# A hybrid decoder layer on one core: the second MLP product in seven block products instead of eight, and a low part made by an adding DMA

## The chip, the cores and the metric

The kernel runs on one core of one Trainium2 chip. The metric is the device time in microseconds of one execution. The time before is the median of three runs, 508.71 us (508.6 to 509.68). The profile is of a single execution.

## The reference, cut to what matters

One layer of a decoder trunk on 256 tokens of width 1024, in float32: a combined input projection, a convolution branch and a sparse attention branch with gates, a cross-attention over 256 memory tokens, and an MLP with squared ReLU. The change touches the MLP:

```
h = h + CrossAttn(RMSNorm(h), RMSNorm(mem))      # 4 heads over N_MEM memory tokens
hf = _rmsnorm(h, norm_ffn_g) @ w_ff1             # (256, 1024) @ (1024, 4096)
h = h + jnp.square(jax.nn.relu(hf)) @ w_ff2      # (256, 4096) @ (4096, 1024)
return _rmsnorm(h, norm_final_g)
```

## The kernel before, in words

**Products in three parts.** TensorE multiplies most operands in the format fp32r. Each operand is split into a high part (a copy in fp32r, by ScalarE) and a low part (the rest, subtracted by VectorE), and a product that stands for the float32 one is the sum of three: high x high, high x low, low x high (`mm3`, line 322).

**The stream of weights.** All weights lie in HBM in chunks of 128 x 2048 floats (1 MB) in the order of `STREAM` (line 38): after the cross-attention come first-product chunks 0 and 1, then alternately first-product chunk i + 2 and second-product chunk i. SP loads them (`load`, line 185) into three buffers, `raw`. Each chunk is split in two halves of 1024 columns: `high` (line 211) allocates a high and a low tile from two pools of `HALVES` = 6 buffers and puts out ScalarE's copy; its `low` puts out VectorE's subtraction, and after the second half loads the next chunk. `split_high` (line 227) starts a half only while fewer than `HALVES - held[0]` are prepared and unused, and `weights` (line 238) hands a prepared half to the product that needs it.

**The order of the work.** The whole order is written by the program: each engine executes its instructions in the order in which Python puts them out. The helper `Counted` (line 66) adds up a price for each instruction of TensorE, VectorE and ScalarE, and `split_ahead`, `meanwhile` and `tick` (lines 252 to 297) use these sums to decide when to put out the next high part, low part or waiting job. Jobs that take several steps are generators, which `tick` advances one step each. All instructions of these engines carry line 87, the line of the helper.

**The MLP.** `f2` holds the scaled input, transposed, in high and low parts (tile name ff). `ff1(c)` (line 1273) computes 256 of the 4096 hidden features as two tiles of 128 features x 256 tokens (`form_b`, `tile_b`, lines 327 to 349). In the wide form that is used here one matmul of 512 columns multiplies the high weights by the high and low input side by side, and one of 256 columns the low weights by the high input, for each of 8 steps: 16 matmuls a tile. The PSUM banks (tile ps_f) rotate over four. `activation` (line 1260): ScalarE copies one half of the bank to ft, VectorE adds the other, squares with ReLU, ScalarE copies the high part to fs, VectorE subtracts the low part. `ff2` (line 1291) multiplies: for chunk c, for each of the two 128-row blocks of hidden features, each 128-token half and each 512-column half of the output, three matmuls of 512 columns: 24 a chunk, summed over all 16 chunks in four PSUM banks (ps_ff). The loop at line 1327 puts out first-product chunk c + 2, then second-product chunk c. The last two chunks are multiplied output half by output half, so that adding the residual (h_rm, transposed from h_t by TensorE in four steps of `ff_scale`, line 1240), the final norm and the stores start before the last product is done; the last one is split at column 768 (`edge`). `g_out`, the final gain, is loaded by SP before the MLP.

The convolution earlier in the kernel (lines 564 to 600) already sums some of its taps by DMAs that GpSimd's queue issues with an add (`added`, line 580), of 256 KB each.

Of the kernel before, what the change touches and what calls it, by code (L numbers as in the profile page):

```python
# [16 lines left out]
P = 128  # L17
D = 1024
# [44 lines left out]
EARLY = (3,)  # L63

# [41 lines left out]
def block_kernel(ctx, tc, x, xt, mem, memt, wst, wki, vecs, convw, gout, out):  # L106
# [75 lines left out]
    nload, dma = [0], [0.0]  # L182
    high_jobs, low_jobs = [], []

    def load(cuts=(0, N_CHUNK), before=lambda q: None):
        if nload[0] >= len(STREAM):
            return
        c = nload[0]
        nload[0] += 1
        key = STREAM[c]  # L190
        raw = t8(f"raw{c}", F32, (P, N_CHUNK)) if c in EARLY else raws.tile([P, N_CHUNK], F32, tag="raw", name=f"raw{c}")
        n = KT * NK if key[0] == "ki" else N_CHUNK
        src = wki if key[0] == "ki" else wst[INDEX[key]]
        for q, ns in enumerate(slice(a, min(b, n)) for a, b in zip(cuts, cuts[1:])):
            before(q)
            nc.sync.dma_start(raw[:, ns], src[:, ns])
            dma[0] += 1.3 * (ns.stop - ns.start)
        parts = 1 if key[0] == "ki" else 2
        for q in range(parts):
            ns = slice(q * n // parts, (q + 1) * n // parts)  # L200
            high_jobs.append(lambda ns=ns, q=q, last=q == parts - 1: high(key, c, raw, ns, q, last))

    def load_keys(q):
        if q == 0:
            nload[0] += 1
            whole["xk", 0] = raws.tile([P, N_CHUNK], F32, tag="raw", name="raw0").rearrange("p (k n) -> p k n", k=2 * KT)
        both = whole["xk", 0].rearrange("p (c k) n -> p c k n", c=2)
        src = wst[INDEX["xk", 0]].rearrange("p (c k n) -> p c k n", c=2, k=KT)
        nc.sync.dma_start(both[:, :, 4 * q : 4 * q + 4, :], src[:, :, 4 * q : 4 * q + 4, :])

    def high(key, c, raw, ns, q, last):
        n = ns.stop - ns.start
        hi = highs.tile([P, N_CHUNK // 2], F32R, tag="hi", name=f"hi{c}_{q}")[:, :n]
        lo = lows.tile([P, N_CHUNK // 2], F32R, tag="lo", name=f"lo{c}_{q}")[:, :n]
        act(hi, raw[:, ns], AF.Copy)
        ready = scalar.total + 100

        def low():
            dve.after(ready)
            dve.tensor_tensor(out=lo, in0=raw[:, ns], in1=hi.bitcast(F32), op=ALU.subtract)  # L220
            prepared[(*key, q)] = (hi, lo)
            if last and c not in EARLY:
                load()

        low_jobs.append(low)

    def split_high():
# [8 lines left out]
    nsplit, nused, held = [0], [0], [1]  # L236

    def weights(kind, i, half, kt):

        key = (kind, i, half)  # L240
        while key not in prepared:
            split_high()
# [41 lines left out]
    def tick():  # L284
# [9 lines left out]
        if scalar.total < pe.total - SPARE or len(low_jobs) < 2:  # L294
            split_high()
        dve.total = max(dve.total, pe.total - 2900)
        scalar.total = max(scalar.total, pe.total - 2900)

    nturn, groups, halves, due, later = [0], [], [], [], []

# [577 lines left out]
    def qk(name):  # L878
        return big.tile([P, 2, S], F32, tag="qk", bufs=4, name=name)

    for i in range(4):
        q, k = qk(f"q{i}"), qk(f"k{i}")
# [329 lines left out]
    form_c("xo", 0, dst, ox2, 0)  # L1212
    lows_of = []
# [22 lines left out]
    g_out = t8("g_out", F32, (P, D))  # L1236
    nc.sync.dma_start(g_out, gout.partition_broadcast(P))
    r2 = []

    def ff_scale():  # L1240
# [7 lines left out]
        yield  # L1248
        r2.append(sq_f.by_row([ps_aux(f"ps_ff{rb}")[:, :2] for rb in range(2)], [sq_f.sums[:, 0, :]], -1))
        for rb in range(2):  # L1250
            for hf in range(2):
                yield
                ps = ps_aux(f"ps_hr{rb}{hf}")
                for j in range(4):
                    pe.transpose(ps[:, j * P : j * P + P], h_t[:, 4 * hf + j, rb * P : rb * P + P], ident)
                act(h_rm[:, rb, hf * 512 : hf * 512 + 512], ps, AF.Copy)

    start(ff_scale())

    def activation(ps, ct, sh, sl):  # L1260
        t = w2(f"ft{ct}", F32, (P, S))
        total(t, ps)

        def square():
            dve.scalar_tensor_tensor(out=t, in0=t, scalar=0.0, in1=t, op0=ALU.max, op1=ALU.mult)
            act(sh, t, AF.Copy)

        due.append(square)
        yield
        yield  # L1270
        dve.tensor_tensor(out=sl, in0=t, in1=sh.bitcast(F32), op=ALU.subtract)

    def ff1(c):
        parts = t8(f"fs{c}", F32R, (P, 4, S))
        jobs = []

        def after(ct, ps):
            jobs.append(start(activation(ps, ct, parts[:, ct % 2, :], parts[:, 2 + ct % 2, :])))

        if c == 0:  # L1280
            form_b_late("f1", c, f2, after, (4,), ps_aux)
        else:
            form_b("f1", c, f2, after)
        return parts[:, :2, :], parts[:, 2:, :], jobs

    tags[:] = [("mm", 2), ("mm", 2), ("aux", 2), ("aux", 2)]
    turns[0] = -1
    pending = [ff1(0), ff1(1)]
    dst = [[ps_acc(f"ps_ff{rb}{hf}") for hf in range(2)] for rb in range(2)]

    def ff2(c, k, w, x2, rb, hf, cs=slice(0, 512), ps=None):
        x2 = Parts(*x2[:2])
        rows, cols = slice(rb * P, rb * P + P), slice(hf * 512 + cs.start, hf * 512 + cs.stop)
        first, last = c == 0 and k == 0, c == 15 and k == 1
        if ps is None:
            ps = dst[rb][hf][:, cs]
        else:
            first = c == 14 and k == 0
        mm3(ps, x2.hi(k)[:, rows], x2.lo(k)[:, rows], w[0][:, 0, cols], w[1][:, 0, cols], first, last, cs.start > 0)

    hg = t8("hg", F32, (P, 2, D))
# [3 lines left out]
    def last_sum(rb, ps, lo, hi):  # L1305
        h = h_rm[:, rb, lo:hi]
        dve.scalar_tensor_tensor(out=h, in0=ps, scalar=r2[0][:, rb : rb + 1], in1=h, op0=ALU.mult, op1=ALU.add)
# [8 lines left out]
    def power_of(rb, n, other):  # L1316

        dve.tensor_tensor(out=ss[:, rb, n : n + 1], in0=ss[:, rb, n : n + 1], in1=ss[:, rb, other : other + 1], op=ALU.add)
        raised(rb, n)

# [6 lines left out]
    for c in range(14):  # L1327
        pending.append(ff1(c + 2))
        *x2, jobs = pending.pop(0)
        for job in jobs:  # L1330
            finish(job)
        for k in range(2):
            w = weights("f2", c, k, 1)
            split_ahead()
            for rb in range(2):
                for hf in range(2):
                    ff2(c, k, w, x2, rb, hf)
            tick()
    for *_, jobs in pending:
        for job in jobs:  # L1340
            finish(job)
    ws = {(c, k): weights("f2", c, k, 1) for c in (14, 15) for k in range(2)}

    def last_products(rb, lo, hi, ps=None):
        for (c, k), w in ws.items():
            ff2(c, k, w, pending[c - 14], rb, lo // 512, slice(lo % 512, lo % 512 + hi - lo), ps)

    for hf in range(2):
        lo, hi = 512 * hf, 512 * hf + 512
        last_products(0, lo, hi)  # L1350
        last_sum(0, dst[0][hf], lo, hi)
        squared(0, hf, lo, hi)
        if hf == 1:
            dve.tensor_scalar(ss[:, 0, 0:1], ss[:, 0, 0:1], EPS, None, ALU.add)
        gained(0, lo, hi)
    power_of(0, 1, 0)
    scale = rs[:, 0:1]
    for n, (lo, hi) in enumerate(((0, 352), (352, D))):
        cols = hg[:, 0, lo:hi]
        if n == 0:  # L1360
            act(cols, cols, AF.Copy, scale=scale)
        else:
            dve.tensor_scalar(cols, cols, scale, None, ALU.mult)
        store(0, n, lo, hi)

    last_products(1, 0, 512)
    last_sum(1, dst[1][0], 0, 512)
    squared(1, 0, 0, 512)
    gained(1, 0, 512)
    last_products(1, 512, 768)  # L1370
    edge = ps_aux("ps_edge")[:, :S]
    last_products(1, 768, D, edge)
    last_sum(1, dst[1][1], 512, D)
    squared(1, 1, 512, 768)
    gained(1, 512, 768)
    dve.scalar_tensor_tensor(out=ss[:, 1, 1:2], in0=ss[:, 1, 1:2], scalar=EPS, in1=ss[:, 1, 0:1], op0=ALU.add, op1=ALU.add)
    last_sum(1, edge, 768, D)
    junk = w2("junk_edge")
    dve.tensor_tensor_reduce(out=junk[:, :S], in0=h_rm[:, 1, 768:], in1=h_rm[:, 1, 768:], scale=1.0 / D, scalar=ss[:, 1, 1:2],
# [3 lines left out]
    dve.tensor_scalar(hg[:, 1, 432:768], hg[:, 1, 432:768], scale, None, ALU.mult)  # L1383
    store(1, 1, 432, 768)
    act(hg[:, 1, :432], hg[:, 1, :432], AF.Copy, scale=scale)
    store(1, 0, 0, 432)
    dve.scalar_tensor_tensor(out=hg[:, 1, 768:], in0=h_rm[:, 1, 768:], scalar=scale, in1=g_out[:, 768:], op0=ALU.mult, op1=ALU.mult)
    store(1, 2, 768, D)
# [69 lines left out]
```

## Time and profile before

| | |
|---|---|
| median of 3 runs | 508.71 us |
| the profiled execution | 508.7 us, its span 506.9 us |
| granted TensorE clock, mean | 0.997 |
| TensorE busy | 498.8 us (98%) |
| VectorE busy | 410.6 us (81%) |
| ScalarE busy | 332.8 us (66%) |
| GpSimd busy | 44.0 us (9%) |
| the MLP's products, first to last on the chain | 321.7 to 500.9 us |

How to read it: in the lists, PE is TensorE, PEld its weight loads, DVE VectorE, ACT ScalarE, POOL GpSimd, SP the queue that issues most DMAs. A group of instructions reads "line engine operation out<-in shapes xcount | busy us, mean ns of one | idle us before, and who ended it". A wait reads "who <- what it waited for: us in total, times, longest". In the timeline the first two columns are start and duration in us.

### The profile page before, as it was taken

Reading aid. Unit: us, or ns where it says so; the run is one execution under the profiler, and the core shown is the slowest. Engines: PE = TensorE matmul, PEld = TensorE weight load, DVE = VectorE, ACT = ScalarE, POOL = GpSimd, SP = SyncE. Lnnn points to the kernel's source line nnn. Section 1 sums busy time; section 2 is a strip of 40 time slices with the busy share of each in tenths; the row PEclk is TensorE's granted clock in tenths of the full one; section 3 lists DMA queues with packets and bytes.
Section 4 is the critical chain, followed back from the end, with each engine's and each line's share of the span. In section 5 each row is a group of like instructions: output and inputs, shape, how many; then the busy total and the mean of one; then the engine's idle time right before and its main releaser. Section 6 shows DMA issues by size and latency. Waiting matters only on the chain.

```text
span 506.9 us, 7744 instructions
## 1 busy us (share of the span) xinstructions
PE 498.8 (98%) x2893; PEld 439.1 (87%) x2893; DVE 410.6 (81%) x795; ACT 332.8 (66%) x605; POOL 44.0 (9%) x64
## 2 busy tenths in 40 slices
PE   8999999999999999999999999999999999999995
PEld 6999999888889898888888888988888888888884
DVE  4989999999999998798999984787765666665555
ACT  4867666887889977887768474666544454545432
POOL 1001122232323210000000000000000000000000
PEclk9999999999999999999999999999999999999998
DMA  8968869999999984474755444344655545555302
GB/s 295 390 264 254 245 170 214 235 262 254 295 270 278 232 221 167 154 261 143 273 172 198 173 171 177 149 166 167 248 187 221 174 165 180 222 185 195 133 0 83
DMA packets 20869, 104.50 MB, mean 206 GB/s; under 512 B 2400, under 2 KB 3040, under 8 KB 10464
## 3 DMA queue, kind: packets, MB, share of 16 engines
q1 hardware_dynamic: 14496, 92.83, 51.5%
q0 software_dynamic: 5904, 10.75, 12.1%
q8 instruction: 22, 0.36, 0.3%
q10 hardware_dynamic: 432, 0.44, 0.2%
q14 instruction: 15, 0.12, 0.1%
HBM read 92.21 MB, written 1.05 MB: 184 GB/s over the span
## 4 chain that ended last, share of the span: by engine, by line
PE 97%; issue 1%; DVE 0%; ACT 0%; POOLq 0%; POOL 0%; DVEq 0%
PE ps_f L87 18%; PE ps_ff L87 16%; PE ps_conv L87 9%; PE ps_ao L87 4%; PE ps_mix L87 4%; PE ps_co L87 4%; PE ps_ga L87 4%; PE ps_k L87 4%; PE ps_gc L87 4%; PE ps_q L87 4%; PE ps_v L87 4%; PE ps_xo L87 3%; PE ps_xk L87 3%; PE ps_xq L87 2%; PE ps_qi L87 2%; PE ps_xv L87 2%
## 5 line engine op out<-in xcount | busy, mean ns | idle before, releaser
L87 DVE TENSOR_TENSOR lo<-raw,hi 128x1024 fp32r<-128x1024 f32 x163 | 196.9, 1215 | 3.4 <-ACT hi L87 3.4
L87 ACT ACTIVATE hi<-raw 128x1024 fp32r<-128x1024 f32 x163 | 169.9, 1049 | 25.5 <-PE ps_ff L87 18.4
L87 PE MATMUL ps_ff<-hi,fs 128*128 128x512 f32 (+1 forms) x256 | 80.6, 387 | 0.0
L87 PE MATMUL ps_f<-ff,hi 128*128 128x512 f32 x256 | 64.4, 392 | 0.0
L87 DVE SCALAR_TENSOR_TENSOR acc<-u,cw,acc 128x249 f32<-128x249 f32 (+17 forms) x150 | 62.6, 467 | 0.0
L87 DVE TENSOR_TENSOR ft<-ps_f,ft 128x256 f32<-128x256 f32 x32 | 13.6, 424 | 53.1 <-ACT ft L87 53.0
L87 PEld LDWEIGHTS ps_ff<-hi,fs 128*128 128x128 f32 x256 | 47.9, 188 | 9.4
L87 PEld LDWEIGHTS ps_f<-ff,hi 128*128 128x128 f32 x256 | 46.6, 188 | 8.7
L87 PE MATMUL ps_ff<-lo,fs 128*128 128x512 f32 (+1 forms) x128 | 49.5, 387 | 0.0
L87 PE MATMUL ps_conv<-n,hi 128*128 128x256 f32 x256 | 46.6, 284 | 0.0
L580 POOL DMA_DIRECT2D added<-prod x41 | 35.7, 870 | 120.9 <-ACT prod L87 46.5
L87 PEld LDWEIGHTS ps_conv<-n,hi 128*128 128x128 f32 x256 | 39.9, 192 | 0.8 <-issue 0.7
L87 ACT ACTIVATE prod<-u,cw 128x226 f32<-128x226 f32 (+10 forms) x82 | 35.0, 475 | 5.0 <-DMA added<-prod 5.0
L87 PEld LDWEIGHTS ps_f<-ff,lo 128*128 128x128 f32 x256 | 35.2, 190 | 2.7
L87 PE MATMUL ps_conv<-n,lo 128*128 128x256 f32 x128 | 36.2, 283 | 0.0
L87 PE MATMUL ps_f<-ff,lo 128*128 128x256 f32 x256 | 36.0, 282 | 0.0
L87 ACT ACTIVATE fs<-ft 128x256 fp32r<-128x256 f32 x32 | 13.4, 419 | 31.1 <-DVE ft L87 31.1
L87 PEld LDWEIGHTS ps_ff<-lo,fs 128*128 128x128 f32 x128 | 24.1, 188 | 4.3
L87 ACT ACTIVATE ft<-ps_f 128x256 f32<-128x256 f32 x32 | 12.2, 380 | 20.6 <-PE ps_f L87 19.4
L87 PEld LDWEIGHTS ps_conv<-n,lo 128*128 128x128 f32 x128 | 24.6, 192 | 0.0
L87 PE MATMUL ps_v<-hi,n 128*128 128x512 f32 x64 | 19.9, 389 | 0.0
L1322 POOL TENSOR_TENSOR rs_o<-ss_o,half 128x1 f32<-128x1 f32 x2 | 1.1, 558 | 214.5 <-DVE ss_o L87 214.5
(244 smaller groups left out, 891.5 us busy)
## 6 DMA issues: line engine op xcount, KB each, us to landing
raw<-in_wst_dram SPq DMA_DIRECT2D x79, 1024.0 KB, 4.9
added<-prod POOLq DMA_DIRECT2D x41, 256.0 KB, 8.6
raw<-in_wst_dram SPq DMA_DIRECT2D x6, 512.0 KB, 8.9
mem_t<-in_memt_dram SPq DMA_DIRECT2D x2, 512.0 KB, 5.2
x_rm<-in_x_dram SPq DMA_DIRECT2D x2, 512.0 KB, 8.4
mem_rm<-in_mem_dram SPq DMA_DIRECT2D x1, 1024.0 KB, 5.1
mem_t<-in_memt_dram SPq DMA_DIRECT2D x1, 1024.0 KB, 7.1
h_t<-in_xt_dram SPq DMA_DIRECT2D x1, 1024.0 KB, 8.0
```

The costliest lines, as they stand in the source:

```text
L87: return fn(*args, **kwargs)
L580: nc.gpsimd.dma_start(added[:, ts, :].rearrange("p t n -> p (t n)"), prod[:, self.n, :, :].rearrange("p t n -> p (t n)"), accum_op=ALU.add)
L1322: nc.gpsimd.tensor_tensor(out=rs[:, rb : rb + 1], in0=ss[:, rb, n : n + 1], in1=half[:, 0:1], op=ALU.pow)
```

## The change: seven block products for eight, and an adding DMA

Second-product chunks 0 to 13 are seen as 2 x 2 blocks on both sides: the activations as two token halves by two feature blocks (128 x 128 each), the weights as two feature blocks by two column halves (128 x 512 each). Winograd's form of Strassen's scheme makes the four output blocks from seven block products, whose factors are sums and differences of blocks. The sums over all chunks are kept as seven PSUM banks (`sums`), and combined once, after chunk 13. The last two chunks stay plain.

- *Weights.* `load(second=True)` loads these chunks into a buffer of another pool (t8), apart from the other stream. `seven_factors` prepares them: three raw blocks are split in high and low parts (`units`), VectorE forms four differences in place (`forms`), and these are split (`formed`). All of it is on ScalarE and VectorE, nothing on GpSimd.
- *Activations.* `Left`: ScalarE applies ReLU to the bank, then squares into x; VectorE forms four sums of 128 x 128; ScalarE copies the seven blocks' high parts (896 columns), VectorE subtracts their low parts.
- *First product.* All its tiles are in the narrow form: 24 matmuls of 256 columns instead of 8 of 512 and 8 of 256. From chunk 3 on all tiles go to the one bank `front`, the eighth. Half a chunk's matmuls of the second product come between two tiles.
- *Adding DMA.* For the second half of first-product chunks 4 to 15 and the first half of second-product chunk 14, ScalarE writes minus the high part into the low tile, and GpSimd's queue issues a DMA that adds the raw half to it, in place of VectorE's subtraction.
- *Halves in flight.* Five from the start of the MLP as before; two between chunk 0 and the last of the seven-product chunks.
- *The planner.* High-part jobs of the MLP are skipped while their load is not expected to have landed, and `tick` puts out as many jobs as the sums allow.
- *Order at both ends.* The transposes to h_rm and the scale move to separate steps at the start of the MLP; `g_out` is loaded at the end; the seven sums are combined while the last two chunks are multiplied; the split product becomes columns 0 to 255 of the second token half.

The diff, cut to its core:

```diff
+SEVEN = 14
+LANDED = 1500
+BY_DMA = {("f1", i, 1) for i in range(4, 16)} | {("f2", 14, 0)}
...
         act(hi, raw[:, ns], AF.Copy)
         ready = scalar.total + 100
+        if (*key, q) in BY_DMA:
+            act(lo, hi.bitcast(F32), AF.Copy, scale=-1.0)
+            nc.gpsimd.dma_start(lo.bitcast(F32), raw[:, ns], accum_op=ALU.add)
+            dma[0] += 3000
...
+    def seven_factors(i, c, raw, landed):
+        b = raw.rearrange("p (b n) -> p b n", n=512)
+        made = {}
+        def forms(a):
+            if a == 0:
+                dve.tensor_tensor(out=b[:, 0:2, :], in0=b[:, 1:4:2, :], in1=b[:, 0:2, :], op=ALU.subtract)
+            else:
+                dve.tensor_tensor(out=b[:, 3, :], in0=b[:, 3, :], in1=b[:, 0, :], op=ALU.subtract)
+                dve.tensor_tensor(out=b[:, 2, :], in0=b[:, 2, :], in1=b[:, 3, :], op=ALU.subtract)
+            made[a] = dve.total + 100
+        def units(a):
+            bs = slice(0, 1) if a == 0 else slice(2, 4)
...
+            act(hi, b[:, bs, :], AF.Copy)
+            ready = scalar.total + 100
+            def low():
+                dve.after(ready)
+                dve.tensor_tensor(out=lo, in0=b[:, bs, :], in1=hi.bitcast(F32), op=ALU.subtract)
+                prepared["f2", i, a] = (hi, lo)
+            low_jobs.append(low)
+            if a == 1:
+                low_jobs.extend((lambda: forms(0), lambda: forms(1)))
+        def formed(a):
...
+                made["hi"], made["lo"] = (t8(f"{n}{i}", F32R, (P, 4, 512)) for n in ("th", "tl"))
...
+            act(hi, b[:, bs, :], AF.Copy)
...
+                dve.tensor_tensor(out=lo, in0=b[:, bs, :], in1=hi.bitcast(F32), op=ALU.subtract)
+                prepared["f2", i, 2 + a] = (hi, lo)
+                if a == 1:
+                    load(second=True)
...
+        for a in range(2):
+            high_jobs.append((lambda a=a: units(a), 2, i - 1, lambda: landed, c))
+        for a in range(2):
+            high_jobs.append((lambda a=a: formed(a), 3, i - 1, lambda a=a: made.get(a, 1e9), c))
+
+    def split_high(force=False):
+        for j, (job, n, start, when, c) in sorted(enumerate(high_jobs), key=lambda j: j[1][4]):
+            if n == 1 and nsplit[0] - nused[0] >= HALVES - held[0] or n == 2 and nsplit[1] - nused[1] >= 2 or multiplied[0] < start:
+                continue
+            if when and not force and when() > max(scalar.total, pe.total) + 400:
+                continue
+            high_jobs.pop(j)
...
+        def rectified(self, k, ps):
+            t = w2(f"ft{self.c}{k}", F32, (P, S))
+            act(t, ps[:, :S], AF.Relu)
...
+            x = self.x
+            act(x[:, 0::7, :] if k == 0 else x[:, 1:3, :], t.rearrange("p (r n) -> p r n", r=2), AF.Square)
...
+            for dst, one, other, op in ((3, a21, a22, ALU.add), (5, a11, a21, ALU.subtract),
+                                        (4, x[:, 3, :], a11, ALU.subtract), (6, a12, x[:, 4, :], ALU.subtract)):
+                dve.tensor_tensor(out=x[:, dst, :], in0=one, in1=other, op=op)
...
+            act(self.h, x[:, :7, :], AF.Copy)
...
+            dve.tensor_tensor(out=self.l, in0=x[:, :7, :], in1=self.h.bitcast(F32), op=ALU.subtract)
...
+    held[0] = HALVES - 2
+    sums = {n: ps_acc(f"ps_ff{n}") for n in (1, 2, 3, 5)}
+    sums.update({n: ps_mm(f"ps_ff{n}") for n in (6, 7)})
+    sums[4] = ps_aux("ps_ff4")
+    front = ps_aux("ps_f")
+    LEFT = {1: 0, 2: 1, 3: 6, 4: 2, 5: 3, 6: 4, 7: 5}
+    RIGHT = {1: (0, 0), 2: (1, 0), 3: (1, 1), 5: (2, 0), 7: (2, 1), 6: (3, 1), 4: (3, 0)}
...
+    for c in range(SEVEN):
+        ready_left(c)
+        w = {}
+        for part, ns in enumerate(((1, 2, 3), (5, 7, 6, 4)) if c < SEVEN - 1 else ((1, 2, 3), (6, 7, 5, 4))):
+            if 0 < c < 14:
+                ff1_tile(c + 2, part, front)
+            for a in range(2):
+                w[2 * part + a] = factors(c, 2 * part + a)
+            split_ahead()
...
+            for n in ns:
+                product(c, n, w)
+            if part == 1:
+                multiplied[0] = c + 1
+            meanwhile()
+            tick()
...
+    act(u2s, sums[1], AF.Copy)
+    add_to(0, 0, 512, sums[1])
+    dve.tensor_tensor(out=u2s, in0=sums[6], in1=u2s, op=ALU.add)
+    dve.tensor_tensor(out=u3s, in0=sums[7], in1=u2s, op=ALU.add)
+    add_to(0, 512, D, u2s)
...
+    add_to(1, 512, D, sums[5])
+    add_to(0, 512, D, sums[5])
```

More of the change, by code (lines that the diff above doesn't have):

```diff
@@ L181, in block_kernel, with by_blocks, load @@
     prepared, whole = {}, {}
-    nload, dma = [0], [0.0]
+    toload, dma = list(STREAM), [0.0]
+    def by_blocks(key):
+        return key[0] == "f2" and key[1] < SEVEN
     high_jobs, low_jobs = [], []
-    def load(cuts=(0, N_CHUNK), before=lambda q: None):
-        if nload[0] >= len(STREAM):
+    def load(cuts=(0, N_CHUNK), before=lambda q: None, second=False):
+        if not any(by_blocks(key) == second for key in toload):
             return
[L188 to L191, printed above, removed]
+        key = toload.pop(next(j for j, key in enumerate(toload) if by_blocks(key) == second))
+        c = STREAM.index(key)
+        raw = t8(f"raw{c}", F32, (P, N_CHUNK)) if c in EARLY or second else raws.tile([P, N_CHUNK], F32, tag="raw", name=f"raw{c}")
         n = KT * NK if key[0] == "ki" else N_CHUNK
@@ L197, in load @@
             dma[0] += 1.3 * (ns.stop - ns.start)
+        if key[0] == "f2" and key[1] < SEVEN:
+            seven_factors(key[1], c, raw, dma[0] + LANDED)
+            return
         parts = 1 if key[0] == "ki" else 2
@@ L295, in tick @@
             split_high()
+        while seven and low_jobs and dve.total < pe.total - SPARE:
+            split_low()
+        while seven and scalar.total < pe.total - SPARE and split_high():
+            pass
         dve.total = max(dve.total, pe.total - 2900)
@@ L299, in block_kernel @@
     nturn, groups, halves, due, later = [0], [], [], [], []
+    seven = []
     def fill_one():
@@ L1212, in block_kernel @@
     form_c("xo", 0, dst, ox2, 0)
+    load(second=True)
     lows_of = []
@@ L1235, in block_kernel, with ff_rows @@
     h_rm = t8("h_rm", F32, (P, 2, D))
-    g_out = t8("g_out", F32, (P, D))
-    nc.sync.dma_start(g_out, gout.partition_broadcast(P))
+    pass
     r2 = []
+    def ff_rows():
+        for rb in range(2):
+            for hf in range(2):
+                yield
+                ps = ps_acc(f"ps_hr{rb}{hf}")
+                for j in range(4):
+                    pe.transpose(ps[:, j * P : j * P + P], h_t[:, 4 * hf + j, rb * P : rb * P + P], ident)
+                act(h_rm[:, rb, hf * 512 : hf * 512 + 512], ps, AF.Copy)
     def ff_scale():
@@ L1247, in ff_scale @@
         yield
[L1248 to L1251, printed above, removed]
-                yield
[L1253 to L1284, printed above, removed]
+        r2.append(sq_f.by_row([ps_mm(f"ps_ffs{rb}")[:, :2] for rb in range(2)], [sq_f.sums[:, 0, :]], -1))
@@ L1286, in block_kernel, with ff1_tile @@
+    lefts = []
+    def ff1_tile(c, k, ps):
+        if k == 0:
+            lefts.append(Left(c))
+        w = weights("f1", c, k, KT)
+        split_ahead()
+        tile_b(ps, w, f2, wide=False)
+        meanwhile()
+        lefts[c].read(k, ps)
+        tick()
+    seven.append(True)
     tags[:] = [("mm", 2), ("mm", 2), ("aux", 2), ("aux", 2)]
     turns[0] = -1
[L1288 to L1299, printed above, removed]
+    lefts.append(Left(0))
@@ new lines, in block_kernel @@
+    held[0] = 3
+    load(second=True)
+    form_b_late("f1", 0, f2, lambda k, ps: lefts[0].read(k, ps), (4,), ps_aux, False)
+    for c in (1, 2):
+        for k in range(2):
+            ff1_tile(c, k, ps_turn(f"ps_f{c}{k}"))
+    finish(rowed)
+    finish(scaled)
+    held[0] = HALVES - 2
[4 more added lines that the diff above has]
+    LEFT = {1: 0, 2: 1, 3: 6, 4: 2, 5: 3, 6: 4, 7: 5}
@@ L1301, in block_kernel @@
+    plain = range(SEVEN, 16)
+    ws = {}
+    held[0] = 1
+    for c in plain:
+        ready_left(c)
+        ws.update({(c, k): weights("f2", c, k, 1) for k in range(2)})
+    g_out = t8("g_out", F32, (P, D))
+    nc.sync.dma_start(g_out, gout.partition_broadcast(P))
     hg = t8("hg", F32, (P, 2, D))
@@ new lines, in block_kernel, with last_products @@
+    add_to(0, 512, D, u2s)
+    dve.scalar_tensor_tensor(out=h_rm[:, 1, :].rearrange("p (b n) -> p b n", b=2), in0=u3s.unsqueeze(1).to_broadcast([P, 2, 512]),
+                             scalar=r2[0][:, 1:2], in1=h_rm[:, 1, :].rearrange("p (b n) -> p b n", b=2), op0=ALU.mult, op1=ALU.add)
+    add_to(1, 512, D, sums[5])
+    add_to(0, 512, D, sums[5])
+    def last_products(rb, lo, hi, ps, first=False):
+        rows = slice(rb * P, rb * P + P)
+        for c, k in ws:
+            x, y = lefts[c].plain, ws[c, k]
+            mm3(ps, x[0][:, k, rows], x[1][:, k, rows], y[0][:, 0, lo:hi], y[1][:, 0, lo:hi],
+                first and c == SEVEN and k == 0, c == 15 and k == 1, True)
```

179 lines of the change are left out of this document (114 added, 65 removed).

## Prediction

> **What bounds the kernel now.** I read the page first (busy time, then the chain), then the stages in the table of windows, then the chain in order of time, and last the durations, waits and DMA rows that the sum needs.
>
> ```profile
> span 506.9 us, 7744 instructions
> PE 498.8 (98%) x2893; PEld 439.1 (87%) x2893; DVE 410.6 (81%) x795; ACT 332.8 (66%) x605; POOL 44.0 (9%) x64
> ...
> PE 97%; issue 1%; DVE 0%; ACT 0%; POOLq 0%; POOL 0%; DVEq 0%
> PE ps_f L87 18%; PE ps_ff L87 16%; PE ps_conv L87 9%; PE ps_ao L87 4%; PE ps_mix L87 4%; PE ps_co L87 4%; PE ps_ga L87 4%; PE ps_k L87 4%; PE ps_gc L87 4%; PE ps_q L87 4%; PE ps_v L87 4%; PE ps_xo L87 3%; PE ps_xk L87 3%; PE ps_xq L87 2%; PE ps_qi L87 2%; PE ps_xv L87 2%
> ```
>
> The chain is TensorE for 97% of the span, and a third of the span is the MLP (ps_f, ps_ff). The windows of the MLP, columns as in the head of that view: start:end and length, then busy time of PE, weight loads, DVE, ACT, POOL, then granted clock, DMA share, GB/s.
>
> ```profile
> 321.73:357.33 35.60, 35.60 (x198) 30.77 (x197) 29.49 (x51) 23.29 (x40) 0.00 (x0) 1.00 0.47 172
> 357.33:484.21 126.88, 126.88 (x649) 108.54 (x649) 79.24 (x114) 65.21 (x93) 0.00 (x0) 1.00 0.52 184
> 484.21:506.90 22.69, 16.49 (x84) 13.93 (x83) 11.77 (x23) 5.68 (x13) 1.12 (x2) 0.94 0.13 46
> ```
>
> From 321.73 to 484.21 TensorE is busy without a gap at full clock, VectorE for 29.49 of 35.60 and then 79.24 of 126.88 us. So time is gained here only by fewer or shorter matmuls, and it is kept only if VectorE, ScalarE and the DMAs still deliver operands at the new pace. One pair of chunks (a first-product chunk, a second-product chunk) stands in the chain as
>
> ```profile
> 368.38 5.56 PE ps_f L87 x32
> 373.94 5.47 PE ps_ff L87 x24
> ```
>
> that is 11.03 us a pair, and a 512-column matmul is 5.47 / 24 = 0.228 us.
>
> **The matmuls: the gain.** In 14 chunks of the second product, 7 block products of 3 matmuls replace 8: 3 x 0.228 = 0.684 us less a chunk, 9.6 us in all. Against this, the first product turns narrow: per 128 output features, 24 matmuls of 256 columns instead of 8 of 512 and 8 of 256, with a weight load for each. The same three-matmul group with 256 columns stands in the cross-attention output:
>
> ```profile
> 316.05 0.28 PE L87 MATMUL ps_xo<-ox,lo 128*128 128x256 f32 x1
> 316.17 0.40 PE L87 MATMUL ps_xo<-ox,hi 128*128 128x256 f32 x2
> 316.41 0.28 PE L87 MATMUL ps_xo<-ox,lo 128*128 128x256 f32 x1
> ```
>
> One group starts 0.36 us after the other, 0.12 us a matmul, so the weight loads stay hidden at this width. A chunk costs 48 x 0.12 = 5.76 us against 5.56: 0.2 us more, 3.2 us over 16 chunks. Net -6.4 us on TensorE; a pair takes 5.76 + 21 x 0.228 = 10.55 us. The transposes of h_t and the sums of squares move ahead of the products but are the same instructions, the last two chunks keep their plain 48 matmuls, and the end of the kernel its one split product: nothing.
>
> **VectorE: is there room?** Two starts in a row, from the timeline:
>
> ```profile
> 398.77 1.23 DVE L87 TENSOR_TENSOR lo<-raw,hi 128x1024 fp32r<-128x1024 f32 x1
> 399.91 0.42 DVE L87 TENSOR_TENSOR fs<-ft,fs 128x256 fp32r<-128x256 f32 x1
> 400.24 1.22 DVE L87 TENSOR_TENSOR lo<-raw,hi 128x1024 fp32r<-128x1024 f32 x1
> ```
>
> In a queue that never empties, 1024 elements take 1.14 us and 256 take 0.33, hence about 0.20 for 128, 0.60 for 512, 1.00 for 896. Per pair in the changed kernel: first product, one low part of two (the other goes by DMA), 1.14. Second product: low parts of the raw blocks 0.60 + 1.14, the four block differences 1.14 + 2 x 0.60, their low parts 2 x 1.14, together 6.36. Activations: four sums of 128 and one low part of 896, 1.80. Sum 9.3 of 10.55 us, 88%. Before it was 4 x 1.14 + 6 x 0.33 = 6.5 of 11.03. The added 2.8 us lie beside TensorE as long as VectorE idles less than 1.25 us a pair. How much it idles now, and why:
>
> ```profile
> DVE ft L87 <- ACT ft L87: 46.5, 23, 3.2
> ```
>
> 46.5 us in 23 waits over 357 to 484 us, 2.0 us each, all before the addition that the change takes out (ReLU and square now go to ScalarE, and VectorE reads a result a turn later). A queue with more work waits less. The kernel has a stage that shows it:
>
> ```profile
> 36.50:187.00 150.50, 150.50 (x951) 135.15 (x950) 147.96 (x345) 118.75 (x243) 39.01 (x46) 1.00 0.92 243
> ```
>
> There VectorE was busy 147.96 of 150.50 us with ScalarE at 79% and the DMA engines at 0.92, and TensorE lost nothing. But part of that VectorE work was taps that nothing waits for soon; in the MLP every item has a due time. I take no stall in the steady pairs.
>
> **The start of the MLP** is tighter. Before chunk 2, VectorE must do two second-product chunks: 2 x (6.36 - 2 x 1.14) = 8.2 us on top of 29.49, less 0.8 for lighter activations and less some 3.4 for three first-product halves that are no longer prepared ahead (five halves in flight become two): 33.5 us in 35.60 - 2 x 0.684 + 4 x 0.2 = 35.0 us. If VectorE keeps the 6.1 us of idle time it has in that window, the loss is 4.6 us; if it closes all gaps, none. I take 2 us, nearer to none, since the new work can fill the gaps.
>
> **ScalarE and the single bank.**
>
> ```profile
> L87 ACT ACTIVATE hi<-raw 128x1024 fp32r<-128x1024 f32 x46 | 48.4, 1052 | 19.4 <-PE ps_ff L87 18.4
> ...
> L87 ACT ACTIVATE fs<-ft 128x256 fp32r<-128x256 f32 x23 | 9.7, 420 | 21.9 <-DVE ft L87 21.9
> ...
> L87 ACT ACTIVATE ft<-ps_f 128x256 f32<-128x256 f32 x23 | 8.8, 384 | 20.4 <-PE ps_f L87 19.4
> ```
>
> Per pair: three passes over first-product halves (two high parts, one negated copy for the adding DMA) 3 x 1.05; high parts of seven blocks 3 x 1.05 and one of 512, about 0.63 (between the two rows); ReLU 2 x 0.38, squares 2 x 0.42, the 896 high part 0.95: 9.5 of 10.55 us by these durations, less in a full queue, where they overlap. It fits. Seven sums take seven of eight PSUM banks, so all first-product tiles share one; a tile's first matmul now waits until ScalarE has read the tile before it. What covers this: nine block matmuls, 9 x 0.228 = 2.05 us, or twelve, 2.7 us. ReLU needs 0.38 of that, so ScalarE may be 1.6 us behind. Queued behind a late ReLU are all later matmuls. I take 0.
>
> **The adding DMA.** For 12 chunks the low part of the second half is made by ScalarE writing minus the high part and GpSimd's queue adding the raw half (512 KB). At most two halves are in flight, so this half is begun when the tile of the same half of the previous chunk starts, and is due one pair later, 10.55 us. The nearest rows are the convolution's, of half that size:
>
> ```profile
> added<-prod POOLq DMA_DIRECT2D x41, 256.0 KB, 8.6
> ```
> ```profile
> L580 POOL DMA_DIRECT2D added<-prod x41: 859/862/1050, 36.5 to 183.1; - x41
> ...
> DMA to landing us min/median/max: 3.8/8.6/11.4
> ```
> ```profile
> q1 hardware_dynamic: 14496, 92.83, 51.5%
> q0 software_dynamic: 5904, 10.75, 12.1%
> ```
>
> (The last two are bytes in MB and share of 16 engines' span.) 12.1% of 506.9 us over 41 is 1.5 us of all engines each; doubling the size adds as much: 5.3, 10.1 or 12.9 us. ScalarE can begin about 1.2 us ahead of that tile's start (2.05 less ReLU and square) and needs 2.1 us, so the data land 0.9 us plus this after the start: 6.2, 11.0 or 13.8 us against 10.55. The median came with the engines at 0.92 and one adding DMA every 150.5 / 41 = 3.7 us, two or three under way together; here there is one a pair, and loads at 0.52 plus 3 us of 10.55, some 0.8. I take 7 us, in the lower half: landed 7.9 us after, 2.7 us to spare. The raw buffer is freed by that DMA instead of VectorE, two loads later; SP's queue carries both streams of loads and would hold the second-product load behind it only if this were late.
>
> The Trainium skill's page "DMA: Bandwidth & Descriptors" (Anatomy of one DMA) fits a DMA on this path as 2.0 us plus bytes over 436 GB/s, 3.2 us for this one by estimate. The trace's shortest, of half the size, took 3.8 us, and its median 8.6. By the page's figure this edit could never stall TensorE, and the total would stay as it is below.
>
> **The end.** Combining seven sums adds to VectorE four scaled additions, two plain ones and one of 1024, beside the 48 last matmuls:
>
> ```profile
> L87 DVE SCALAR_TENSOR_TENSOR h_rm<-ps_ff,ms_ff,h_rm 128x512 f32<-128x512 f32 x4 | 3.0, 747 | 5.1 <-PE ps_ff L87 5.1
> L87 DVE TENSOR_TENSOR hg<-h_rm,g_out 128x512 f32<-128x512 f32 x3 | 2.1, 692 | 0.1
> ```
>
> 4 x 0.75 + 2 x 0.69 + 1.2 = 5.6 us, in the last window where VectorE was busy 11.77 of 22.69 us, and started before the last plain products. The chain after the last matmul keeps its instructions. I take 0, with bounds of -0.5 and +1.
>
> **Sum.** The profiled run took 508.7 us, its span 506.9 us, 1.8 us around it, and the median of the runs is the same 508.71. 508.7 - 9.6 + 3.2 + 2.0 = 504.3 us.
>
> **Rivals.**
> *VectorE becomes the bound.* For it: 88% in steady pairs and 96% at the start, operands that go ScalarE, VectorE, ScalarE, VectorE before a formed block is ready, loads that wait for a buffer that VectorE frees. Against it: the stage at 98%. It decides from 1.25 us of idle time a pair. With 2.0 us, one old wait, a pair takes 11.3: 13 pairs x 0.75 = 10 us, 514 us; with both old waits 13.3 us and 540 us. It eats the gain at 1.75 us. 0.13.
> *The adding DMA lands late.* It costs something from 9.7 us of landing time and eats the gain near 10.2; at 11.4 us it is 12 x 1.7 = 20 us, 524 us. For it the median worked out above, against it the lighter DMA load. 0.13. The Trainium skill's page "SBUF — State Buffer" (SBUF: two separate sides) warns that VectorE in a two-port mode can keep GpSimd from writing descriptors. By that rule this rival would gain. The trace does not bear it out for this mix: 41 issues took 859 to 1050 ns beside a VectorE at 98%.
> *The single bank stalls TensorE.* ScalarE 1 us beyond its 1.6 us once a pair: 13 us, 517 us. For it ScalarE's 9.5 of 10.55 us; against it the overlap in a full queue. 0.07.
> *Small stalls just cancel the gain*, 507.7 to 509.7 us: 0.07.
> *That fewer matmuls are not issued after all* is excluded by the code: 21 per chunk are written out.
>
> **How the numbers follow.** The forecast, TensorE still the bound with 0 to 5 us of start and end losses (501.8 to 507.7), has 0.60. A measurement here can tell about 0.2%, 1 us. Faster takes the forecast and a little of each rival's mild end, 0.62; within 0.2%, 0.08; slower, 0.30. The range goes from 501.8 (no start loss, best end) to 514 (VectorE with one old wait a pair): some 0.16 lies above, 0.03 below.
>
> **What would show it.** Right: tiles of ps_f of 24 matmuls in 2.88 us, 21 matmuls of ps_ff in 4.8 us, pairs of 10.55 us, VectorE near 88%, PE busy without gaps from chunk 2 on. Wrong: TensorE waits named after lo with a DMA (adding), after VectorE lo or fs, or after ScalarE ft at ps_f; pairs over 11.03 us would make it slower.

## The result and the profile after

The changed kernel takes 504.75 us, the median of 7 runs (504.42 to 508.01), beside 509.15 us for 7 runs of the kernel before on the same chip: a ratio of 0.9928, 95% interval 0.9904 to 0.9952. Over all comparisons of this study the median of the kernel before lies between 509.15 and 509.62 us. The profiled execution has a span of 503.1 us, 3.8 us less than before. (The helper's line is now 90.)

The page of the changed kernel, its span, its busy times and the head of its chain:

```profile
span 503.1 us, 8348 instructions
PE 492.4 (98%) x3107; PEld 444.7 (88%) x3107; DVE 452.0 (90%) x835; ACT 377.4 (75%) x666; POOL 55.6 (11%) x77
...
PE 91%; DMA 2%; DVE 2%; ACT 2%; issue 1%; POOLq 0%; POOL 0%; DVEq 0%; SPq 0%
```

TensorE sets the time until near the end, with 6.4 us less work (498.8 to 492.4), and VectorE went from 81% to 90%. The chain has 91% of TensorE where it had 97%, because it leaves TensorE at 466.22 us: from there it runs over ScalarE, the last adding DMA and, from 480.90 us on, mostly VectorE. The windows of the MLP by stage in the changed kernel, and below them one pair of chunks (same columns as in the prediction):

```profile
321.73:357.33 35.60, 35.60 (x261) 33.62 (x261) 33.32 (x56) 30.56 (x50) 0.91 (x1) 1.00 0.56 203
357.33:484.21 126.88, 126.88 (x830) 116.51 (x829) 116.10 (x151) 104.67 (x148) 10.32 (x12) 1.00 0.71 222
484.21:503.10 18.89, 11.27 (x62) 9.63 (x60) 13.27 (x24) 4.67 (x12) 1.12 (x2) 0.93 0.15 56
373.23:383.79 10.56, 10.56 (x72) 9.70 (x71) 9.77 (x14) 8.66 (x13) 0.86 (x1) 1.00 0.77 249
```

TensorE has no gap in the first two stages, although VectorE is busy for 116.10 of 126.88 us where it was 79.24, and ScalarE for 104.67 where it was 65.21. The chain in order of time (start, length, group), first the start of the MLP, then a steady pair:

```profile
342.02 4.91 PE ps_ff L90 x21
346.93 2.87 PE ps_f L90 x24
349.80 2.31 PE ps_ff L90 x9
...
373.23 2.87 PE ps_f L90 x24
376.10 2.75 PE ps_ff L90 x12
378.85 2.87 PE ps_f L90 x24
381.72 2.07 PE ps_ff L90 x9
```

A pair is 2.87 + 2.75 + 2.87 + 2.07 = 10.56 us; the forecast had 10.55. At the start one group of nine matmuls takes 2.31 us where the later ones take 2.07: 0.24 us is what the start of the MLP lost, too little to show as a gap in the window. The longest waits of the changed kernel from 357 to 484 us:

```profile
POOL lo L228 <- ACT ft L90: 115.9, 11, 18.6
ACT ft L90 <- PE ps_f L90: 21.1, 12, 2.0
...
DVE tl L90 <- ACT th L90: 5.8, 12, 1.1
```

The wait of 46.5 us before VectorE's addition is gone with that addition. No row of TensorE is in this list: it waited neither for the single bank nor for an adding DMA. ScalarE, which reads the bank, waits for TensorE's tiles instead (21.1 us).

**Where the 3.8 us are.** Four pieces, each between two rows that both kernels have:

| piece | before | after | difference |
|---|---|---|---|
| start of the span to the first matmul of ps_conv | 21.38 | 22.32 | +0.94 |
| from there to the start of the last matmul | 479.04 | 472.88 | -6.16 |
| from there to the start of VectorE's last instruction | 2.36 | 3.03 | +0.67 |
| from there to the end of the span | 4.12 | 4.87 | +0.75 |

So the products gained 6.16 us (by the forecast's terms and the loss at the start 9.6 - 3.2 - 0.24), and 2.4 us went elsewhere. The third piece stands in the timelines of the end (start, duration, instruction, idle before). Before:

```profile
500.42 0.28 PE L87 MATMUL ps_edge<-hi,fs 128*128 128x256 f32 x1
...
500.79 0.48 DVE L87 SCALAR_TENSOR_TENSOR h_rm<-ps_edge,ms_ff,h_rm 128x256 f32<-128x256 f32 x1
```

After, with the first and the last work on the seven sums, and then the last matmul and what is ahead of its addition:

```profile
485.04 0.75 DVE L90 SCALAR_TENSOR_TENSOR h_rm<-ps_ff,ms_ff,h_rm 128x512 f32<-128x512 f32 x1
...
489.13 2.07 DVE L90 SCALAR_TENSOR_TENSOR h_rm<-ps_ff,ms_ff,h_rm 128x512 f32<-128x512 f32 x3
...
495.20 0.28 PE L90 MATMUL ps_ff<-hi,fs 128*128 128x256 f32 x1
...
495.62 0.42 DVE L90 TENSOR_TENSOR hg<-h_rm,g_out 128x256 f32<-128x256 f32 x1
496.17 0.16 DVE L90 SCALAR_TENSOR_TENSOR ss_o<-ss_o 128x1 f32<-128x1 f32 x1
496.24 0.48 DVE L90 SCALAR_TENSOR_TENSOR h_rm<-ps_ff,ms_ff,h_rm 128x256 f32<-128x256 f32 x1
```

The last addition started 0.37 us after the last matmul and now starts 1.04 us after it: the sums hold VectorE until 491.20, the additions of the plain products come behind them, and two other instructions are still ahead of the last one in the queue. The fourth piece goes with an extra transfer; the DMA rows of the changed kernel's last 4 us have one packet that the last 4 us before do not have:

```profile
q14 instruction: 1, 0.01, 0.9%
```

Of the fourteen profiles of this study, the ten with such a packet at their end need 4.47 to 5.47 us from VectorE's last instruction to the end, the four without it 4.10 to 4.16. The four are exactly the kernels without adding DMAs in the MLP: the kernel before, its variant with the narrow first product, and the two variants of the changed kernel below that have no adding DMA there. So the 0.75 us seem to be a price of the adding DMAs; what the packet is for stays open. The first piece has the same instructions in both kernels; it lies between 21.29 and 22.46 us in the profiles. The kernel before and its variant have 21.38 and 21.61. The changed kernel has 22.32, 22.06 and 22.02; of its nine variants two have 21.29 and 21.59, the others 21.92 to 22.46. That speaks for some addition by the change, but with two profiles on one side and this spread on the other it is not shown.

### The profile page after: what moved, and what is told of

It reads as the page before. It is cut to its first block, busy times and chain, and to the rows that moved or that the text cites. A ratio compares the mean times of both kernels' runs of the same rounds, so it can differ in the third digit from the quotient of the medians.

```text
span 503.1 us, 8348 instructions
## 1 busy us (share of the span) xinstructions
PE 492.4 (98%) x3107; PEld 444.7 (88%) x3107; DVE 452.0 (90%) x835; ACT 377.4 (75%) x666; POOL 55.6 (11%) x77
## 4 chain that ended last, share of the span: by engine, by line
PE 91%; DMA 2%; DVE 2%; ACT 2%; issue 1%; POOLq 0%; POOL 0%; DVEq 0%; SPq 0%
PE ps_f L90 17%; PE ps_ff L90 12%; PE ps_conv L90 9%; PE ps_ao L90 4%; PE ps_mix L90 4%; PE ps_co L90 4%; PE ps_ga L90 4%; PE ps_k L90 4%; PE ps_gc L90 4%; PE ps_q L90 4%; PE ps_v L90 4%; PE ps_xo L90 3%; PE ps_xk L90 3%; PE ps_xq L90 2%; PE ps_qi L90 2%; PE ps_xv L90 2%
## 5 line engine op out<-in xcount | busy, mean ns | idle before, releaser
L90 ACT ACTIVATE hi<-raw 128x1024 fp32r<-128x1024 f32 (+1 forms) x163 | 161.5, 1010 | 9.0 <-DVE acc L90 3.6
L90 PE MATMUL ps_f<-ff,hi 128*128 128x256 f32 x512 | 93.6, 284 | 0.0
L90 PEld LDWEIGHTS ps_f<-ff,hi 128*128 128x128 f32 x512 | 81.5, 192 | 2.0
L90 PE MATMUL ps_f<-ff,lo 128*128 128x256 f32 x256 | 72.5, 283 | 0.0
L90 DVE TENSOR_TENSOR tl<-raw,th 128x1024 fp32r<-128x1024 f32 x28 | 34.1, 1222 | 5.8 <-ACT th L90 5.8
L90 DVE TENSOR_TENSOR raw<-raw 128x512 f32<-128x512 f32 (+1 forms) x42 | 36.4, 867 | 0.9
L90 PE MATMUL ps_ff<-th,fs 128*128 128x512 f32 x112 | 37.0, 391 | 0.0
L90 PE MATMUL ps_ff<-hi,fs 128*128 128x512 f32 (+1 forms) x116 | 36.6, 377 | 0.0
L90 ACT ACTIVATE th<-raw 128x1024 fp32r<-128x1024 f32 x28 | 28.1, 1046 | 1.5 <-DVE raw L90 1.5
L90 PEld LDWEIGHTS ps_ff<-th,fs 128*128 128x128 f32 x112 | 21.1, 188 | 4.1
L90 PEld LDWEIGHTS ps_ff<-hi,fs 128*128 128x128 f32 x116 | 21.4, 189 | 3.6
```

The costliest lines, as they stand in the source:

```text
L90: return fn(*args, **kwargs)
```

## The experiments

Each is one edit of one of the two kernels; the medians stand beside runs of the kernel before on the same chip.

**The terms of the sum, one by one.** The kernel before with the narrow first product alone:

```diff
-        total(t, ps)
+        act(t, ps[:, :S], AF.Copy)
...
-            form_b("f1", c, f2, after)
+            form_b("f1", c, f2, after, False)
```

> The kernel before with only the narrow first product: 24 matmuls of 256 columns a tile, ScalarE copying the bank, and no addition of its halves on VectorE. If TensorE is the bound and the narrow form costs 24 x 0.12 us a tile, the time is 509.15 + 3.2 = 512.3 us and a first-product chunk takes 5.76 us on the chain instead of 5.56. Rival, that the narrow form costs nothing because it only fills waiting time: 509 us.

Measured: 512.33 us beside 509.62, ratio 1.006 (1.0042 to 1.0079). Its chain:

```profile
380.62 5.75 PE ps_f L87 x48
386.38 5.47 PE ps_ff L87 x24
```

5.75 us a chunk for 5.56: the term of +3.2 us holds. Next, the changed kernel with one block product too many (number 4 is multiplied twice in all 14 chunks):

```diff
             if part == 1:
+                product(c, 4, w)
+            if part == 1:
```

> The changed kernel with block product 4 multiplied twice in each of the 14 chunks, so eight products again (the output is not the reference's), everything else the same. If TensorE sets the pace of the pairs: 504.75 + 14 x 0.684 = 514.3 us, pairs of 11.24 us. Rival, that VectorE or ScalarE sets the pace and TensorE has room: 507 us or less.

Measured: 513.92 us beside 509.62, ratio 1.0099 (1.0071 to 1.0127). Its chain:

```profile
397.64 2.87 PE ps_f L90 x24
400.51 3.43 PE ps_ff L90 x15
```

15 matmuls take 3.43 us for 2.75 with twelve: 0.68 us a chunk, 9.5 us over 14, as the 9.6 of the sum. Both terms of TensorE are thereby shown.

**VectorE and the adding DMA.** The changed kernel with all low parts back on VectorE:

```diff
-BY_DMA = {("f1", i, 1) for i in range(4, 16)} | {("f2", 14, 0)}
+BY_DMA = set()
```

> The changed kernel without the adding DMAs: VectorE subtracts all low parts, 9.3 + 1.14 = 10.4 us a pair of 10.55. If VectorE's queue keeps full and TensorE is still the bound: 504.75 to 508 us. Rival, that VectorE is already at its limit at 9.3 us because each pair carries about 1.25 us or more of waiting: at least 14 x 1 us more, 517 us and above.

Measured: 508.69 us (10 runs) beside 509.62, ratio 0.9988 (0.9978 to 0.9998): above the first theory's range, and far from the rival's 517 us. The windows of the stage, of an early and of a later pair, and the one wait of a matmul in the stage:

```profile
357.00:484.00 127.00, 125.65 (x815) 113.81 (x814) 124.70 (x163) 92.15 (x130) 0.00 (x0) 1.00 0.46 170
396.06:406.62 10.56, 10.56 (x72) 9.69 (x71) 10.46 (x15) 7.82 (x12) 0.00 (x0) 1.00 0.47 163
428.00:438.80 10.80, 10.80 (x71) 9.68 (x71) 10.70 (x15) 7.92 (x12) 0.00 (x0) 1.00 0.48 198
```
```profile
PE ps_f L90 <- ACT ft L90: 1.3, 1, 1.3
```

The loss has three parts. Some 1.9 us are lost up to and in the second tile of chunk 4, at 364.12 us: TensorE waits for ScalarE to read the single bank, and ScalarE had waited 2.4 us for VectorE's differences. Then the pairs take 10.56 us with VectorE busy for 10.46, and nothing is lost; but the six pairs from 417.21 us on take 10.80 us with VectorE busy for 10.70, 1.4 us in all. Why VectorE's same 15 instructions take longer there stays open. And the end is later: VectorE's last instruction starts 4.17 us after the last matmul, for 3.03. So one subtraction of 1024 elements a pair, 1.14 us, is enough to make VectorE the bound, and of the gain of 4.4 us 0.9 are left. The adding DMA, a small part of the diff, carries most of what the change is worth. The next kernel goes further, and also subtracts the low part of the second half of the chunks from 4 on twice:

```diff
+            for _ in range(2 if key[0] == "f1" and key[1] > 3 and q == 1 else 1):
+                dve.tensor_tensor(out=lo, in0=raw[:, ns], in1=hi.bitcast(F32), op=ALU.subtract)
```

> As e3_no_dma, and VectorE subtracts the low part of the second half of the 12 later first-product chunks twice: 11.6 us of VectorE a pair, over TensorE's 10.55. If a full queue works without gaps: 12 x 1.05 = 12.6 us more, some 517 us, VectorE at 99% in the pairs. Rival, waits of 1 to 2 us a pair on top: 530 us and above.

Measured: 528.31 us beside 509.62, ratio 1.0373 (1.0349 to 1.0398), between the two and nearer to the dearer one. Its waits and its window:

```profile
PEld ps_ff L90 <- DVE tl L90: 8.4, 5, 2.3
...
PE ps_ff L90 <- ACT th L90: 5.6, 3, 1.9
```
```profile
357.00:484.00 127.00, 114.11 (x695) 101.64 (x694) 121.72 (x154) 79.67 (x113) 0.00 (x0) 0.94 0.41 155
```

VectorE is busy for 96% and not for all of it, because operands pass between it and ScalarE, and TensorE waits for either. Twelve subtractions more, 13.7 us by estimate from 1.14 each, cost 19.6 us: beyond the limit, time is lost faster than VectorE's own work grows. Part of it may be slower matmuls, since the granted clock is 0.94 in this stage, for 1.00; this run does not separate the two. The opposite edit sends both halves of the first-product chunks 4 to 15 through the adding DMA:

```diff
-BY_DMA = {("f1", i, 1) for i in range(4, 16)} | {("f2", 14, 0)}
+BY_DMA = {("f1", i, q) for i in range(4, 16) for q in range(2)} | {("f2", 14, 0)}
```

> Both halves' low parts of first-product chunks 4 to 15 by adding DMA: VectorE 1.14 us a pair less, ScalarE 1.05 us more (10.5 of 10.55 us by the durations, 9.2 in a full queue), two adding DMAs a pair. If TensorE is the bound with room on the others: 504.75 within 0.7 us, pairs of 10.56 us. Rival, ScalarE or the DMA engines at their limit: pairs over 10.8 us, 507.5 us and above.

Measured: 517.69 us beside 509.5, ratio 1.015 (1.0102 to 1.0197): the expectation failed. Its waits, its window and the landing of its adding DMAs (360 to 480 us):

```profile
PEld ps_f L90 <- DMA lo<-raw: 8.5, 6, 2.5
PE ps_f L90 <- DMA lo<-raw: 7.3, 6, 2.3
```
```profile
357.00:484.00 127.00, 119.67 (x757) 109.05 (x756) 95.39 (x134) 107.09 (x144) 18.95 (x22) 0.98 0.95 265
```
```profile
DMA to landing us min/median/max: 4.8/7.0/10.4
```

VectorE has room now (95.39 of 127), but the DMA engines are at 0.95 and an adding DMA takes 7.0 us, up to 10.4. TensorE waits for it by name. After a first landing of 9.9 us, the time grows through the stage: 5.0 us for the issue at 367.26 us, 7.0 for the one at 409.99, 10.4 for the one at 469.31. Of TensorE's 7.3 us of waiting, 7.1 come after 427 us. Over steady pairs the DMA engines are at 0.55 without the adding DMAs (374.94 to 459.36 us of the kernel without them) and at 0.77 with one a pair (373.23 to 457.71 us of the changed kernel), so two ask for 0.99 by estimate: the engines are full, and transfers fall behind from pair to pair. ScalarE, the other candidate of the rival, is busy for 40.21 of 53 us from 431 us on, where TensorE waits. This is the rival "the adding DMA lands late", one more transfer a pair away from the change.

How near it is with one transfer a pair is seen in the changed kernel itself. Its ScalarE around one such step, GpSimd's issue, and the landing times of the 13 adding DMAs:

```profile
403.62 1.99 ACT L90 ACTIVATE th<-raw 128x1024 fp32r<-128x1024 f32 x2
405.51 1.57 ACT L90 ACTIVATE hi<-raw 128x512 fp32r<-128x512 f32 x2
407.12 1.06 ACT L90 ACTIVATE lo<-hi 128x1024 fp32r<-128x1024 f32 x1
```
```profile
408.47 0.86 POOL L228 DMA_DIRECT2D lo<-raw  x1 [9.70 <-ACT ft L90]
```
```profile
L228 POOL DMA_DIRECT2D lo<-raw x13: 859/859/912, 346.7 to 476.2; - x13
...
DMA to landing us min/median/max: 4.5/4.9/6.8
```

The issues come in the order of the chunks, the first for chunk 4. The sixth, at 408.47, is therefore chunk 9's, whose second tile begins at 415.47 (one pair of 10.56 us after the tile at 404.91; the first such tile, chunk 4's, begins at 362.67). The limit is thus 7.0 us of landing time. With the median of 4.9 us it would land at 413.4, 2.1 us ahead (it took 4.6). The longest of the twelve first-product transfers took 5.5 us, 1.5 ahead; the 6.8 us belong to the thirteenth, of second-product chunk 14.

**A fifteenth chunk by seven products:**

```diff
-SEVEN = 14
+SEVEN = 15
```

(and chunk 14 leaves the set of the adding DMA).

> Seven block products in 15 of 16 chunks, one plain chunk left at the end. TensorE has 0.684 us less. If the end is VectorE's (it has no gap from 481 us to the end in the changed kernel's profile and reaches the last sum 0.7 us after TensorE): one more chunk of factors on VectorE and only 5.5 us of plain products beside the combining of the sums, 1 to 4 us slower than 504.75, 506 to 509 us. Rival, that the end has room: 504.1 us.

Measured: 511.04 us (10 runs) beside 509.5, ratio 1.0015 (0.9989 to 1.004), more than either theory. The window of its end, and TensorE's waits there:

```profile
484.00:503.00 19.00, 14.50 (x60) 11.27 (x58) 18.00 (x24) 6.75 (x13) 0.57 (x1) 0.91 0.03 10
```
```profile
PE ps_ff L90 <- DVE tl L90: 2.2, 1, 2.2
...
PE ps_ff L90 <- ACT th L90: 1.3, 1, 1.3
```

VectorE is busy for 18.00 of 19.00 us and TensorE for 14.50. Both waits are for the formed factors of the fifteenth chunk and end at 489.34 and 492.00 us, while VectorE's first addition of a sum starts only at 491.86. So the factors come late first, and combining the sums then follows late beside one plain chunk. From 492 to 502 us the granted clock is 0.83, so the remaining matmuls are slower too.

**The end.** Four edits try to bring back the 0.67 us of the third piece. Two give products with the final gain to GpSimd, those of the first token half, and all but one:

```diff
-        dve.tensor_tensor(out=hg[:, rb, lo:hi], in0=h_rm[:, rb, lo:hi], in1=g_out[:, lo:hi], op=ALU.mult)
+        (nc.gpsimd if rb == 0 else dve).tensor_tensor(out=hg[:, rb, lo:hi], in0=h_rm[:, rb, lo:hi], in1=g_out[:, lo:hi], op=ALU.mult)
```

> The changed kernel, the multiplication of the first token half by the final gain (two of 128x512) on GpSimd instead of VectorE. If VectorE's lag of 0.7 us behind TensorE at the end is what the end loses: 504.1 us. Rival, GpSimd slows VectorE beside it or is late itself: 504.75 us or more.

> As e7_pool_gain, with the first 512 columns of the second half's gain on GpSimd too: VectorE 2.1 us less in all. If the lag was VectorE's, nothing more is won than in e7_pool_gain, 504.1 us, with VectorE idle before the last sum. Rival, GpSimd in the way: slower than e7_pool_gain.

Measured: 505.39 us beside 509.5, ratio 0.9916 (0.9885 to 0.9947), and 504.76, ratio 0.9896 (0.9863 to 0.9929). Neither is told from the changed kernel, and by the pieces neither mends the end: from the last matmul to VectorE's last instruction 3.34 and 3.16 us, for 3.03. Two rows of the first one's timeline, which overlap, show a reason:

```profile
491.43 2.55 POOL L1487 TENSOR_TENSOR hg<-h_rm,g_out 128x512 f32<-128x512 f32 x2 [14.27 <-DVE h_rm L90]
```
```profile
492.79 1.21 DVE L90 SCALAR_TENSOR_TENSOR ss_o<-ss_o 128x1 f32<-128x1 f32 x1 [0.79 <-ACT junk_o L90]
```

A VectorE instruction on one column takes 1.21 us, 0.16 in the changed kernel, and ends as GpSimd's product ends. The Trainium skill's page "SBUF — State Buffer" (SBUF: two separate sides) says that the two engines share a port pair and that one holding it exclusively blocks the other; these rows agree. The third edit moves one product with the gain, and the store behind it, to the very end:

```diff
-        gained(0, lo, hi)
+        if hf == 0:
+            gained(0, lo, hi)
...
+    gained(0, 512, D)
```

> The changed kernel; the gain of the first token half's columns 512 to 1023 (0.69 us of VectorE) is multiplied after the last sum's reduction, in VectorE's 0.67 us of waiting for GpSimd's power, and its scaling and store follow. If VectorE's lag of 0.7 us behind TensorE is what the end loses: 0.5 to 0.7 us less than the changed kernel run beside it, the last sum 0.4 us after TensorE's last matmul. Rival, the late store of 256 KB takes its place: the same or slower.

Measured: 505.36 us beside 509.38, ratio 0.9912 (0.9898 to 0.9926): missed. VectorE used the freed time to wait 0.79 us for ScalarE's sum of squares further up, and its last instruction, now behind the moved product, starts 3.42 us after the last matmul. From there to the end it takes 5.47 us, the longest of all profiles, as the rival with the late store had it. Beside it, on the same chip, the changed kernel unchanged:

> The changed kernel itself, beside e9_late_gain and against the kernel before: 504.75 us, and its first convolution matmul 0.7 to 1 us later than in the kernel before if that shift belongs to the kernel, at any time between if it is one run's chance.

Measured: 504.13 us, ratio 0.9895 (0.9881 to 0.9908); the first convolution matmul starts at 22.06 us, 0.68 later than in the kernel before. The fourth edit changes only the order of the last instructions:

```diff
-    gained(1, 256, 512)
-    dve.scalar_tensor_tensor(out=ss[:, 1, 1:2], in0=ss[:, 1, 1:2], scalar=EPS, in1=ss[:, 1, 0:1], op0=ALU.add, op1=ALU.add)
     add_to(1, 0, 256, edge)
+    dve.scalar_tensor_tensor(out=ss[:, 1, 1:2], in0=ss[:, 1, 1:2], scalar=EPS, in1=ss[:, 1, 0:1], op0=ALU.add, op1=ALU.add)
...
     raised(1, 2)
+    gained(1, 256, 512)
```

> The changed kernel with two of VectorE's instructions of the end put behind the last addition: the addition of the last (split) product is put out ahead of the gain for columns 256 to 511 of the second token half and of the sum of the squares' parts, and that gain goes behind the issue of GpSimd's power. Theory: the last 0.67 us between the last matmul and its addition are VectorE's queue, so the addition follows the last matmul by 0.4 us instead of 1.04, the sum of the squares' parts then waits for ScalarE until about 1.0 us after the last matmul, and the reduction behind it starts 0.5 us earlier than now: 0.5 us less than the unchanged changed kernel in the same call, 504.2 beside 504.75. Rival: ScalarE's part of the squares is late by as much, or the gain no longer fits into the 0.67 us in which VectorE waits for GpSimd: within 0.2 us of the unchanged one.

> The changed kernel unchanged, beside the run with the addition moved: 504.1 to 504.75 us, the last addition about 1.0 us after the last matmul.

Measured: 504.25 us, ratio 0.9922 (0.9896 to 0.9947), and unchanged 504.46, ratio 0.9925 (0.9899 to 0.995), beside 509.2. By the medians the two are the same. The timeline of the edited one:

```profile
494.49 0.28 PE L90 MATMUL ps_ff<-hi,fs 128*128 128x256 f32 x1
```
```profile
494.13 1.33 DVE L90 SCALAR_TENSOR_TENSOR h_rm<-ps_ff,ms_ff,h_rm 128x512 f32<-128x512 f32 x2
495.45 0.16 DVE L90 SCALAR_TENSOR_TENSOR ss_o<-ss_o 128x1 f32<-128x1 f32 x1
495.64 0.48 DVE L90 CUSTOM_DVE_ANT_0 junk_edge<-h_rm,ss_o 128x256 f32<-128x256 f32 x1
...
496.05 0.42 DVE L90 TENSOR_TENSOR hg<-h_rm,g_out 128x256 f32<-128x256 f32 x1
```

The reduction starts 1.15 us after the last matmul, for 1.55 in the changed kernel (496.75 - 495.20) and 0.88 in the kernel before. So the order in the queue is shown as the cause of 0.40 of the 0.67 us; the rest is not shown. Of these 0.40 us, 0.28 reach VectorE's last instruction (2.75 us after the last matmul, for 3.03), since GpSimd's power, now beside a product on VectorE, takes 0.68 us for 0.56. That is a gain of the trace which the medians cannot tell from none.

## Why the prediction was right

The forecast was 504.3 us with TensorE still the bound, and 504.75 were measured, with 6.4 us less of TensorE's work as the sum had it.

**The matmuls**: right in both terms and their sum. Minus 9.6 and plus 3.2 were forecast; the middle piece lost 6.16 us, start of the MLP included, and each term was measured alone.

**The start of the MLP**: mis-sized. The forecast took 2.0 us out of bounds of 0 to 4.6; the trace has 0.24, one wait of a weight load for a low part. VectorE closed nearly all of its gaps: 33.32 of 35.60 us, where the forecast had counted 33.5 us of work.

**The end**: mis-sized. "I take 0, with bounds of -0.5 and +1": it cost 0.67 us up to VectorE's last instruction, of which the order of VectorE's queue behind the sums (485.04 to 491.20) is shown for 0.40, and 0.75 us behind it, together above the upper bound. The forecast looked for room in the average of the window (11.77 of 22.69 us), not at the last microseconds of the queue.

**The first 22 us** were not thought of: +0.94 us in this pair of profiles, of which an unknown part is chance. The errors, -1.8 at the start of the MLP against +0.7, +0.75 and +0.9, nearly cancel. That the total came within 0.5 us is in this part luck.

**VectorE's room**: right in its result, with less to spare than thought: 9.77 of 10.56 us busy in a pair, 92%, where 88% were forecast. An instruction that stands alone lasts longer (1.23 us) than the start-to-start price (1.14), so a busy time in a queue with gaps is longer than the sum of such prices. Without the adding DMA the prices give 9.3 + 1.14 = 10.44 us a pair; 10.46 were measured in the early pairs and 10.70 in the later ones.

**The adding DMA**: the verdict was right, and its steps were off in both directions. Landing was taken at 7 us and took 4.9. The Trainium skill's fit on "DMA: Bandwidth & Descriptors" (Anatomy of one DMA) gave 3.2 us by estimate; the shortest here is 4.5. But ScalarE was thought to begin 1.2 us ahead of the tile's start; it has copies of the second product's blocks in front (the rows from 403.62 on), and the DMA is issued 3.6 us after that start (404.91), not 0.9. So the spare time is 2.1 us at the median and not 2.7, and the rival decides from 7.0 us of landing, not from 9.7. (The points at which two rivals eat the gain, 1.75 us of idle time and 10.2 us of landing, were reckoned with 6.4 us; with the forecast's own gain of 4.4 they are 1.59 and 10.07.)

**The single bank and ScalarE**: right, nothing lost. **The rival that VectorE becomes the bound** did not come true in the steady pairs, but it is near: the kernel without the adding DMA shows it, and there the single bank holds TensorE up once, for 1.3 us.

## What to carry to other kernels

When matmuls are traded for work on other engines, price that work per steady pair: the gain is TensorE's alone as long as every engine stays under the pair, and here a single subtraction of 1.14 us in 10.56 decided over most of it. Look for the loss at the two ends, instruction by instruction and in the queue's order, since the share of a window says nothing about what stands ahead of the last instruction. Of a transfer that replaces an instruction, count from its issue, behind the whole queue of the engine that prepares it, to its due time; add up the load of the DMA engines per pair; and try it doubled: two per pair were already too many.

## What the runs showed of the hardware that was not expected

- The same adding DMA of 512 KB takes 4.9 us (median) with one a pair and the DMA engines at 0.71. With two a pair, at 0.95, it takes 7.0 us (median), and from the second issue on the time grows from 5.0 to 10.4 in the course of the stage. The convolution's DMAs of half that size, one every 3.7 us at 0.92, took 8.6: here the load counted for more than the size.
- A product on GpSimd over two operands in SBUF makes a VectorE instruction beside it take 1.21 us for 0.16. A VectorE addition that reads PSUM, beside the same product, was not lengthened: four such additions in a row take 2.73 us there, three take 2.07 in the changed kernel.
- One instruction packet at the end of a program goes with some 0.8 us more between the last VectorE instruction and the end of the span (4.87 for 4.12 us). It is there in the ten profiles of kernels with adding DMAs in the MLP, and in none of the four others.
